# Attention's value products in three-half PSUM buffers, with a new order of the pieces

## The chip, the cores and the metric

The kernel runs on one core of one Trainium2 chip. What counts is the device time of one execution in microseconds (us), lower being better. All times below come from runs on the chip and from one execution that the hardware profiler recorded.

## What is computed

One layer of a decoder trunk for 1024 prompt tokens and 8 sample tokens with 1024 channels: a mixer (pooling and convolution), cross-attention to 256 memory tokens with 4 heads of 256 channels, and a gated feed-forward part. The change lies in the cross-attention:

```python
def cross_attn(h, k, v, w_q, w_o):
    B, L, _ = h.shape
    q = (h @ w_q).reshape(B, L, MEM_HEADS, MEM_HEAD_DIM)
    s = jnp.einsum('blhd,bmhd->bhlm', q, k).astype(jnp.float32) / math.sqrt(MEM_HEAD_DIM)
    p = jax.nn.softmax(s, axis=-1).astype(v.dtype)
    o = jnp.einsum('bhlm,bmhd->blhd', p, v).reshape(B, L, D_MODEL)
    return o @ w_o
```

The sample tokens have keys and values of their own (a cache), and the prompt's are computed from `mem_prompt`.

## The kernel before, in words

**Precision.** Each operand of a matmul is held as a pair, a rounded high part and a low part (the rest). A product is three passes (`PASSES`: high by high, high by low, low by high) into one PSUM accumulation. So a product's result leaves PSUM twice: ScalarE (ACT) copies it to the high part, and then VectorE (DVE) subtracts that copy from the same PSUM data to make the low part.

**Stages of the attention.** Letters name the pieces in the string `ORDER`, and a digit follows each. `q` is the query projection of 128 channels (72 matmuls, tile `ps`). `S` is the scores of 256 tokens of one head (12 matmuls into one bank, tile `sc`), with the softmax: maximum on DVE, exponentials on ACT, normalisation on GpSimd (POOL) or DVE (tile `probs`). `T` transposes four 128x128 blocks of probabilities on the TensorE (PE; tile `pt`), and ACT and DVE split them into the pair `pT`. `P` is the value product: `P`n makes output channels 128n to 128n+127 of the attention from head n//2 (tile `pv`, line 1083 on), in two halves of 512 tokens, c = 0 and 1. A half is six matmuls into one bank (lines 1091 to 1095). ACT's copy is line 1098 and DVE's subtraction line 1099, and both write halves of the pair `oo`n. `a`, `b`, `c`, `d`, `e` do the same for the samples without the PE's matmuls: DVE multiplies cache rows (`spcache_k`, `spcache_v`) by broadcast rows (`sbcache_k`, `sbcache_v`), which pass through DRAM (`qd` for queries, `pd` for the probabilities `prow`), and POOL writes the samples' columns of `oo` (lines 375 and 384). `o` is the output projection (tile `po`, line 485), which reads all eight `oo`.

**PSUM.** [...] Two buffers of three banks each (tag `mm`) serve `ps`, `pv`, `po` and some of the `sc`, in turn, and two of one bank each (tag `ms`) serve `pt`, most `sc` and small sums. A `pv` buffer holds the two halves of one `P`, so one of its three banks stays empty.

**Order.** Every piece adds tasks to a list, with what each reads and writes (`Program.add`). For PSUM those keys are finer than a tile: `(ps, c)` is one half. `Program.order` then plans all engines with costs of its own and writes the instructions out in the planned order; each engine runs its instructions in that order. The string `ORDER` sets the tasks' priorities, so a new string moves instructions on every engine. The waits between engines are put in by the layer below, which sees the instructions one after another in the planned order, with the tiles that they touch.

Of the kernel before, what the change touches and what calls it, by code (L numbers as in the profile page):

```python
# [10 lines left out]
AF = mybir.ActivationFunctionType  # L11
ALU = mybir.AluOpType
AX = mybir.AxisListType

P = 128
# [25 lines left out]
ORDER = (  # L41
# [5 lines left out]
)  # L47

# [5 lines left out]
ALL_SAMPLES = (1, 6, 7)  # L54

SCORES_MM = (12, 13, 14, 15)
SLACK = {"Pool": 0.3, "ACT": 0.15, "DVE": 0.05, "PE": 0.05}


# [16 lines left out]
A12, A22, S4, S1, A11, S2, S3 = range(7)  # L76
# [27 lines left out]
class Program:  # L104
# [10 lines left out]
    def add(self, engines, emit, r=(), w=(), lock=False, func=None, nbytes=0):  # L115
        t = Task()
        t.engines = {}
        for e, cost in engines.items():
            factor, more = self.margin.get(e, (1, 0)) if not nbytes else (1, 0)
            t.engines[e] = cost * factor + more  # L120
        t.emit, t.lock, t.func, t.nbytes = emit, lock, func, nbytes
        t.prio = len(self.tasks) + self.later
        if "PE" not in engines and any(isinstance(x[0], Buf) and x[0].tag in ("mm", "ms") for x in r):
            t.prio += BIAS["evac"]
        deps = set()
        for x in r:
            if x in self.writer:
                deps.add(self.writer[x])
        for x in w:
            if x in self.writer:  # L130
                deps.add(self.writer[x])
            deps.update(self.readers.get(x, ()))
        for x in r:
            self.readers.setdefault(x, []).append(t)
        for x in w:
            self.writer[x], self.readers[x] = t, []
        deps.discard(t)
        t.deps, t.followers, t.ends = deps, [], {}
        t.waiting = len(deps)
        for d in deps:  # L140
            d.followers.append(t)
        t.bufs = list({id(x[0]): x[0] for x in list(r) + list(w) if isinstance(x[0], Buf)}.values())
        self.tasks.append(t)
        return t

    def order(self):
# [48 lines left out]
        while len(issued) < len(self.tasks):  # L195
            best = None
            for e, tasks in open_.items():
                pick, slack = None, SLACK.get(e, 0.02)
                for t in tasks:
# [61 lines left out]
def hybrid_step_kernel(ctx: ExitStack, tc: tile.TileContext, io):  # L261
# [9 lines left out]
    add = pg.add  # L271

    def buf(name, tag, shape, dtype=F32):
        return Buf(name, tag, shape, dtype)

    def op_buf(name, shape=(P, 2, T), dtype=F32):
        return buf(name, "op", shape, dtype)
# [7 lines left out]
    def mm_buf(name, width=3):  # L285
        return buf(name, "mm", (P, width, 512))

    def ms_buf(name):
        return buf(name, "ms", (P, 512))

    def f32(ap):
        return ap.bitcast(F32)
# [8 lines left out]
    def pe(n, count=1):  # L301
        return (0.0135 + 0.000417 * n) * count
# [4 lines left out]
    def act(n, ps=False, ptrs=0):  # L307
        return (0.05 if ps else 0.093) + 0.000833 * n + 0.093 * ptrs

    def dve(n):  # L310
        return 0.065 + 0.00105 * n
# [493 lines left out]
    a2 = [op_buf(f"a{i}") for i in range(2)]  # L805
# [143 lines left out]
    x1 = [op_buf(f"x1_{j}") for j in range(4)]  # L949
# [60 lines left out]
    probs, pT = {}, {}  # L1010
# [8 lines left out]
    def scores(n):  # L1019
# [3 lines left out]
        pr = probs[h]  # L1023
        ps = mm_buf(f"sc{h}_{i2}", 1) if n in SCORES_MM else ms_buf(f"sc{h}_{i2}")
        pk = (ps,)
# [39 lines left out]
    def p_transpose(n):  # L1065
# [7 lines left out]
        def emit(e):  # L1073
# [6 lines left out]
        add({"DVE": dve(512)}, lambda e: e.tensor_tensor(pt[:, 1, sl], ps[:], f32(pt[:, 0, sl]), ALU.subtract),  # L1080
            [(ps,), (pt, 0, t4)], [(pt, 1, t4)])

    def pv(n):
        h, dt = n // 2, n % 2
        ps = mm_buf(f"pv{n}", 2)
        col, v = (h % 2) * 256 + dt * P, vv[h // 2]
        oo = oop[n]
        for c in range(2):
            sl = slice(c * 512, (c + 1) * 512)

            def emit(e, c=c, sl=sl):
                for m in range(2):
                    for p, (vi, pi) in enumerate(PASSES):
                        e.matmul(ps[:, c], v[:, vi, m, col : col + P], pT[h][m][:, pi, sl],  # L1094
                                 start=(m == 0 and p == 0), stop=(m == 1 and p == 2))

            add({"PE": pe(512, 6)}, emit, [(v, 0), (v, 1)] + [(pT[h][m], p, c) for p in range(2) for m in range(2)], [(ps, c)])
            add({"ACT": act(512, True)}, lambda e, c=c, sl=sl: e.activation(oo[:, 0, sl], ps[:, c], AF.Copy), [(ps, c)], [(oo, 0, c)])
            add({"DVE": dve(512)}, lambda e, c=c, sl=sl: e.tensor_tensor(oo[:, 1, sl], ps[:, c], f32(oo[:, 0, sl]), ALU.subtract),  # L1099
                [(ps, c), (oo, 0, c)], [(oo, 1, c)])  # L1100


    def s_query(h):
# [496 lines left out]
    def hidden_load(f):  # L1600
# [9 lines left out]
        "Y": lambda _: state_out("pool_s", st_pool, "pool", 15), "Z": lambda _: state_out("conv_s", st_conv, "conv", 30),  # L1610
        "L": lambda _: layer_norm(), "V": values, "O": pair(out_a), "B": pair(out_b),
        "q": q_group, "f": lambda _: token_factors(), "t": x1_square, "u": x2_square, "S": scores, "T": p_transpose, "P": pv,
        "a": s_query, "b": s_scores, "c": s_softmax, "d": s_values, "e": s_out,
        "o": proj_o, "x": lambda n: plain_block(A12 if n > 3 else A11, n % 4, n // 4, 0), "y": lambda j: plain_block(A22, j, 1, 1), "z": sum_blocks,
# [24 lines left out]
    for u in range(units):  # L1639
        c, p = u // 4, u % 4  # L1640
# [222 lines left out]
```

## Time and profile before

| | us |
|---|---|
| median of 3 runs (1216.54 to 1219.12) | 1217.39 |
| the profiled execution | 1217.88 |
| its span on the profile | 1216.1 |
| PE busy in it | 1198.4 |
| first `pv` matmul | 411.2 |
| first `po` matmul | 447.8 |

The span runs from the first instruction to the last. PE, DVE, ACT and POOL are the engines, PEld the weight loads of the PE, SPq the queue that issues most DMAs. Times in a timeline count from the span's start. "[1.15 <-DVE oo L1099]" behind a row means that the engine had been idle for 1.15 us, and that an instruction of line 1099 on DVE ended this.

### The profile page before, as it was taken

The numbers are of one execution on the slowest core, as the hardware profiler recorded it, in microseconds if no ns is written. First come the engines' busy times: TensorE is split into PE (matmuls) and PEld (weight loads), VectorE is DVE, ScalarE is ACT, GpSimd is POOL, SyncE is SP. The second block draws the span as 40 slices with busy tenths as digits, with TensorE's granted clock in tenths as the row PEclk, the third lists the DMA queues.
The fourth block names the chain that finished last, engine by engine and source line by source line (L and its number), as shares of the span: only waits on it lengthen the run. The fifth ranks groups of instructions, "written<-read, shape, count | busy, mean of one in ns | idle before, by whom it ended". The sixth has DMA issues, their size and how long they took to land.

```text
span 1216.1 us, 19401 instructions
## 1 busy us (share of the span) xinstructions
PE 1198.4 (99%) x7720; PEld 1121.8 (92%) x7720; DVE 930.1 (76%) x1548; ACT 524.7 (43%) x718; POOL 251.4 (21%) x297
## 2 busy tenths in 40 slices
PE   8999999999999999999999999999999999999997
PEld 7999988999999979999999999999999999999886
DVE  7999999766258886679877777777867798879744
ACT  7765656455135533454222322233222355544633
POOL 3568842231111102131000000000000024332101
PEclk9999999999999999999999999999999999999999
DMA  7335677326386774422332233222313597678612
GB/s 289 86 73 116 144 210 223 117 104 207 108 266 205 244 271 150 122 87 66 118 114 80 96 114 111 108 79 97 123 70 105 206 309 216 169 195 222 150 52 89
DMA packets 60170, 179.69 MB, mean 148 GB/s; under 512 B 7792, under 2 KB 11568, under 8 KB 58800
## 3 DMA queue, kind: packets, MB, share of 16 engines
q1 hardware_dynamic: 53824, 157.92, 37.4%
q0 software_dynamic: 6256, 20.54, 9.9%
q8 instruction: 60, 0.98, 0.3%
q14 instruction: 30, 0.25, 0.1%
HBM read 144.66 MB, written 33.78 MB: 147 GB/s over the span
## 4 chain that ended last, share of the span: by engine, by line
PE 78%; DVE 4%; DMA 1%; issue 1%; ACT 1%; POOL 0%; DVEq 0%; SPq 0%; ACTq 0%
PE pr L1339 48%; PE po L485 8%; PE fd L1682 6%; PE ps L485 5%; PE oa L485 4%; PE ob L485 4%; PE sc L1036 1%; DVE spcache_k L1133 1%; PE pv L1094 1%; DMA sbcache_v<-pd 1%; DVE oo L1099 1%; PE kps L860 0%; DVE pT L1080 0%; DMA raw<-in_w_k 0%; DMA pd<-prow 0%
## 5 line engine op out<-in xcount | busy, mean ns | idle before, releaser
L1339 PEld LDWEIGHTS pr<-ab,wTb 128*128 128x128 f32 x1056 | 131.8, 188 | 3.5
L1339 PE MATMUL pr<-ab,wTa 128*128 128x260 f32 x1056 | 133.6, 282 | 0.2 <-DVE su L1355 0.2
L1339 PE MATMUL pr<-ab,wTb 128*128 128x260 f32 x1056 | 133.0, 282 | 0.0
L1339 PEld LDWEIGHTS pr<-ab,wTa 128*128 128x128 f32 x1056 | 130.8, 188 | 2.4 <-DVE su L1355 0.4
L1339 PE MATMUL pr<-ab,wG 128*128 128x512 f32 x528 | 129.3, 393 | 0.0
L1355 DVE TENSOR_TENSOR su<-pr,su 128x520 f32<-128x520 f32 (+1 forms) x112 | 77.7, 695 | 57.9 <-PE pr L1339 57.7
L1339 PEld LDWEIGHTS pr<-ab,wG 128*128 128x128 f32 x528 | 96.3, 188 | 19.7 <-DVE wG L384 0.4
L485 PE MATMUL ps<-xop,w 128*128 128x344 f32 x720 | 114.1, 320 | 0.0
L485 PEld LDWEIGHTS ps<-xop,w 128*128 128x128 f32 x720 | 113.6, 188 | 0.0
L1339 PEld LDWEIGHTS pr<-hb,dV 128*128 128x128 f32 x768 | 98.8, 188 | 4.1
L1339 PE MATMUL pr<-hb,dV 128*128 128x260 f32 x768 | 100.1, 283 | 0.0
L485 PE MATMUL ps<-xq,w 128*128 128x344 f32 x576 | 94.9, 322 | 0.5 <-DMA w<-in_w_q 0.5
L485 PEld LDWEIGHTS ps<-xq,w 128*128 128x128 f32 x576 | 90.8, 188 | 0.9 <-DMA w<-in_w_q 0.8
L485 PEld LDWEIGHTS po<-oo,w 128*128 128x128 f32 x576 | 90.8, 188 | 0.6 <-DVE oo L1099 0.4
L485 PE MATMUL po<-oo,w 128*128 128x344 f32 x576 | 91.3, 320 | 0.0
L694 DVE SCALAR_TENSOR_TENSOR cacc<-glu,vec,cacc 128x511 f32<-128x511 f32 (+14 forms) x116 | 76.9, 744 | 0.0
L1339 PE MATMUL pr<-hb,dW 128*128 128x512 f32 x288 | 74.6, 394 | 0.0
L373 ACT ACTIVATE w<-raw 128x1024 fp32r<-128x1024 f32 (+1 forms) x37 | 34.9, 949 | 86.1 <-PE po L485 24.2
L1682 PE MATMUL fd<-ho,w 128*128 128x260 f32 (+1 forms) x432 | 69.1, 321 | 0.0
L1366 POOL MEMSET su<- 128x16 f32 x22 | 2.5, 112 | 318.9 <-PE pr L1339 267.7
L1682 PEld LDWEIGHTS fd<-ho,w 128*128 128x128 f32 x432 | 62.0, 188 | 6.9 <-issue 0.5
L1339 PE MATMUL pr<-ab,wU 128*128 128x512 f32 x264 | 64.6, 393 | 0.0
(309 smaller groups left out, 2189.2 us busy)
## 6 DMA issues: line engine op xcount, KB each, us to landing
gr<-in_w_gu SPq DMA_DIRECT2D x44, 512.0 KB, 3.7
hb<-su SPq DMA_DIRECT2D x8, 1040.0 KB, 4.6
hs<-hb SPq DMA_DIRECT2D x16, 520.0 KB, 5.1
dr<-in_w_dn SPq DMA_DIRECT2D x16, 512.0 KB, 4.6
spcache_k<-in_cache_k SPq DMA_DIRECT2D x12, 512.0 KB, 5.1
hs<-hb SPq DMA_DIRECT2D x12, 512.0 KB, 5.0
raw<-in_w_in SPq DMA_DIRECT2D x10, 512.0 KB, 3.7
hb<-he SPq DMA_DIRECT2D x8, 520.0 KB, 3.6
```

Of the source, the lines that this page charges most:

```text
L373: e.activation(dst(0), src(), AF.Copy, scale=1.0 if gain is None else gain)
L485: e.matmul(ps[:, c, :CW], w[:, wi, cols], x[:, xi, c * CW : (c + 1) * CW], start=first and p == 0, stop=last and p == 2)
L694: e.scalar_tensor_tensor(acc[h][:, n:], src[:, : HALF - n], w, acc[h][:, n:], ALU.mult, ALU.add)
L1036: e.matmul(bank()[:, i * NMEM : (i + 1) * NMEM], qop[2 * h + dt][:, qi, tt * P : (tt + 1) * P], kk[:, ki, 2 * (h % 2) + dt], start=(dt == ...
L1094: e.matmul(ps[:, c], v[:, vi, m, col : col + P], pT[h][m][:, pi, sl], start=(m == 0 and p == 0), stop=(m == 1 and p == 2))
L1099: add({"DVE": dve(512)}, lambda e, c=c, sl=sl: e.tensor_tensor(oo[:, 1, sl], ps[:, c], f32(oo[:, 0, sl]), ALU.subtract), [(ps, c), (oo, 0, ...
L1133: e.scalar_tensor_tensor(piece[:, b], piece[:, b], 1.0, bc[:, b], ALU.mult, ALU.mult, accum_out=out(m)[:, first + b : first + b + 1])
L1339: e.matmul(bank(c), w[:, wi, cols(j)], xs[0](j, xi)[:, c * n : (c + 1) * n], start=onto is None and j == 0 and p == 0, stop=j == nj - 1 an ...
L1355: from_sums(sums, "DVE", dve, lambda e, src, sl: e.tensor_tensor(as_banks(o(sl), src), src, as_banks(a(sl), src), op), [akey], [okey])
L1366: add({"Pool": 0.12}, lambda e: e.memset(o(), 0.0), [], keys)
L1682: e.matmul(view(i), w[:, wi, col : col + P], hops[k][:, xi, half, lo - half * HALF + i * width // count : lo - half * HALF + (i + 1) * wid ...
```

## The change

The function `pv` no longer takes a buffer for each `P`. It counts halves. The first, second and third of three successive halves go to banks 0, 1 and 2 of one buffer, and the fourth takes the next buffer. After `P1` (the constant `EARLY_PV`), which comes first and alone, the count starts anew. So `P1` has a buffer with two halves, and the other fourteen halves lie in five buffers: three, three, three, three and two, where they had seven. Matmuls, copies and subtractions stay as they were, and as many. `ORDER` is rewritten from `S2` to `P5`, and one piece (`z0`) moves ahead of `o2` behind it.

```diff
-    "S2 q4 q5 a2 Y0 S7 S1 S3 S8 T0 d0 T3 T4 S9 T1 S10 T2 d1 q6 T8 q7 S11 T11 T5 P1 S12 T10 a3 S15 S13 T9 S14 T12 b2 T7 T6 "
-    "T13 b3 T14 T15 c3 c2 d2 P4 e1 e0 P5 P2 P3 P7 d3 P0 e3 P6 e2 o0 u0 o4 o1 o5 x1 u4 u1 u5 h0 x0 x4 y0 o2 z0 x5 h2 h3 u2 "
+    "S2 q5 S3 q4 Y0 S1 T0 d0 a2 T1 S8 S10 S11 T2 T3 d1 q6 S9 q7 T8 S7 P1 T10 T4 b2 T7 a3 T5 S12 S13 T11 T12 S15 e0 T6 S14 "
+    "T14 T13 T9 c2 b3 e1 d2 c3 T15 e2 P2 d3 e3 P4 P0 P3 P7 P6 P5 o0 u0 o4 o1 o5 x1 u4 u1 u5 h0 x0 x4 y0 z0 o2 x5 h2 h3 u2 "
...
+EARLY_PV = 1
...
+    pv_banks = {"next": 0}
+
     def pv(n):
         h, dt = n // 2, n % 2
-        ps = mm_buf(f"pv{n}", 2)
...
         for c in range(2):
             sl = slice(c * 512, (c + 1) * 512)
-
-            def emit(e, c=c, sl=sl):
+            bank = pv_banks["next"] % 3
+            if not bank:
+                pv_banks["ps"] = mm_buf(f"pv{n}_{c}")
+            ps = pv_banks["ps"]
+            pv_banks["next"] += 1
+
+            def emit(e, sl=sl, ps=ps, bank=bank):
                 for m in range(2):
                     for p, (vi, pi) in enumerate(PASSES):
-                        e.matmul(ps[:, c], v[:, vi, m, col : col + P], pT[h][m][:, pi, sl],
+                        e.matmul(ps[:, bank], v[:, vi, m, col : col + P], pT[h][m][:, pi, sl],
                                  start=(m == 0 and p == 0), stop=(m == 1 and p == 2))
...
+        if n == EARLY_PV:
+            pv_banks["next"] = 0
```

The places below show the instructions as they stand in the built programs. A number behind a name tells buffers apart, "x3" is three in a row, and what a row waits for stands in brackets, by the engine whose count it waits on.

**The PE before, `P3` and `P7`.** Each has a buffer of its own (`pv3`, `pv7`), and its two halves are rows of three and three matmuls each.

```order
L1146 MATMUL ss2_4289<-ident_74,ssc_81 8x128
L1094 MATMUL pv3_4294<-pT1_0_3836,vv0_2016 128x512 [waits DVE_49]
L1094 MATMUL pv3_4294<-pT1_0_3836,vv0_2016 128x512 x2
L1094 MATMUL pv3_4294<-pT1_1_4182,vv0_2016 128x512 x3
L1094 MATMUL pv3_4294<-pT1_0_3836,vv0_2016 128x512 x3
L1094 MATMUL pv3_4294<-pT1_1_4182,vv0_2016 128x512 x3
L1094 MATMUL pv7_4322<-pT3_0_4200,vv1_1805 128x512 [waits DVE_49]
L1094 MATMUL pv7_4322<-pT3_0_4200,vv1_1805 128x512 x2
```

Each buffer is begun with a wait for DVE, and the second half has none.

**The PE after the change, the same products and the next.** `pv3_0` holds both halves of `P3` and the first of `P7`, `pv7_1` the second of `P7` and both of `P6`, and `pv5_0` both of `P5`.

```order
L1101 MATMUL pv3_0_4296<-pT1_0_4085,vv0_2016 128x512 x3
L1101 MATMUL pv3_0_4296<-pT1_1_4116,vv0_2016 128x512 x3
L1101 MATMUL pv3_0_4296<-pT3_0_4182,vv1_1805 128x512 [waits Activation_49]
L1101 MATMUL pv3_0_4296<-pT3_0_4182,vv1_1805 128x512 x2
L1101 MATMUL pv3_0_4296<-pT3_1_4212,vv1_1805 128x512 x3
L1101 MATMUL pv7_1_4335<-pT3_0_4182,vv1_1805 128x512 [waits DVE_49]
L1101 MATMUL pv7_1_4335<-pT3_0_4182,vv1_1805 128x512 x2
L1101 MATMUL pv7_1_4335<-pT3_1_4212,vv1_1805 128x512 x3
L1155 MATMUL ss3_4345<-ident_74,ssc_81 8x128 [waits DVE_49,PE_49]
L1155 MATMUL ss3_4345<-ident_74,ssc_81 8x128 [waits DVE_49]
L1101 MATMUL pv7_1_4335<-pT3_0_4182,vv1_1805 128x512 x3
L1101 MATMUL pv7_1_4335<-pT3_1_4212,vv1_1805 128x512 x3
```

A buffer is still begun with a wait for DVE, and its third half now has one for ACT (`pv7_1`'s as well, in the next rows).

**The PE after the change, from the last products to the output projection.** The first row is `pv7_1`'s third half.

```order
L1101 MATMUL pv7_1_4335<-pT3_0_4182,vv1_1805 128x512 [waits Activation_49]
L1101 MATMUL pv7_1_4335<-pT3_0_4182,vv1_1805 128x512 x2
L1101 MATMUL pv7_1_4335<-pT3_1_4212,vv1_1805 128x512 x3
L1101 MATMUL pv5_0_4375<-pT2_0_4025,vv1_1805 128x512 [waits DVE_49]
L1101 MATMUL pv5_0_4375<-pT2_0_4025,vv1_1805 128x512 x2
L1101 MATMUL pv5_0_4375<-pT2_1_4067,vv1_1805 128x512 x3
L1101 MATMUL pv5_0_4375<-pT2_0_4025,vv1_1805 128x512 x3
L1101 MATMUL pv5_0_4375<-pT2_1_4067,vv1_1805 128x512 x3
L486 MATMUL po0_4401<-oo0_4013,w44_3813 128x344 [waits DVE_49]
```

The projection's first matmul waits for DVE, as before, where the two halves ahead of it were those of `P6`; the buffer that it takes is the one that `pv7_1` had, since the two are used in turn.

**DVE after the change, behind the last products.** `sst3` and `prow3` are the softmax of the samples' fourth head, `oo`n the subtractions.

```order
L1106 TENSOR_TENSOR oo7_4342<-pv3_0_4296,oo7_4342 128x512
L1106 TENSOR_TENSOR oo7_4342<-pv7_1_4335,oo7_4342 128x512 [waits Activation_49]
L1171 RECIPROCAL sst3_4355<-sst3_4355 8x1
L1172 TENSOR_SCALAR prow3_4361<-prow3_4361,sst3_4355 8x256 [waits DMAHW2_49,DVE_49]
L1106 TENSOR_TENSOR oo6_4370<-pv7_1_4335,oo6_4370 128x512
L1106 TENSOR_TENSOR oo6_4370<-pv7_1_4335,oo6_4370 128x512 [waits Activation_49]
L1106 TENSOR_TENSOR oo5_4397<-pv5_0_4375,oo5_4397 128x512 [waits Activation_49] x2
```

Before, `prow3` had four subtractions behind it, those of `P0` and `P6`. Now there are four again, `P6` and `P5`, but ahead of it stands the subtraction of a half that shares its buffer with the next two.

More of the change, by code (lines that the diff above doesn't have):

```diff
@@ L1089, in pv @@
             sl = slice(c * 512, (c + 1) * 512)
-            def emit(e, c=c, sl=sl):
+            bank = pv_banks["next"] % 3
[4 more added lines that the diff above has]
+            def emit(e, sl=sl, ps=ps, bank=bank):
                 for m in range(2):
                     for p, (vi, pi) in enumerate(PASSES):
-                        e.matmul(ps[:, c], v[:, vi, m, col : col + P], pT[h][m][:, pi, sl],
+                        e.matmul(ps[:, bank], v[:, vi, m, col : col + P], pT[h][m][:, pi, sl],
                                  start=(m == 0 and p == 0), stop=(m == 1 and p == 2))
[L1097 to L1100, printed above, removed]
+            add({"PE": pe(512, 6)}, emit, [(v, 0), (v, 1)] + [(pT[h][m], p, c) for p in range(2) for m in range(2)], [(ps, bank)])
+            add({"ACT": act(512, True)}, lambda e, sl=sl, ps=ps, bank=bank: e.activation(oo[:, 0, sl], ps[:, bank], AF.Copy), [(ps, bank)], [(oo, 0, c)])
+            add({"DVE": dve(512)}, lambda e, sl=sl, ps=ps, bank=bank: e.tensor_tensor(oo[:, 1, sl], ps[:, bank], f32(oo[:, 0, sl]), ALU.subtract),
+                [(ps, bank), (oo, 0, c)], [(oo, 1, c)])
+        if n == EARLY_PV:
+            pv_banks["next"] = 0
     def s_query(h):
```

## The prediction

> **What bounds the kernel now.** I read the page's busy times first, then a table of stretches around the attention, then PE's waits, and last the timeline of the stretch in which the `pv` products run.
>
> ```profile
> span 1216.1 us, 19401 instructions
> PE 1198.4 (99%) x7720; PEld 1121.8 (92%) x7720; DVE 930.1 (76%) x1548; ACT 524.7 (43%) x718; POOL 251.4 (21%) x297
> core 0: us, PE busy (x) PEld busy (x) DVE busy (x) ACT busy (x) POOL busy (x), PEclk, DMA share, GB/s
> 375.00:411.00 36.00, 36.00 (x259) 35.81 (x258) 29.27 (x110) 16.68 (x40) 5.29 (x8) 1.00 0.61 200
> 411.00:426.00 15.00, 14.57 (x101) 12.55 (x100) 13.19 (x34) 12.15 (x31) 2.11 (x7) 1.00 0.88 291
> 426.00:434.00 8.00, 8.00 (x43) 6.59 (x42) 6.81 (x24) 4.35 (x8) 0.00 (x0) 1.00 0.14 53
> 434.00:448.00 14.00, 12.62 (x55) 9.33 (x54) 11.31 (x35) 5.76 (x13) 0.00 (x0) 1.00 0.89 325
> 448.00:460.00 12.00, 12.00 (x77) 12.00 (x78) 9.68 (x49) 1.05 (x2) 0.87 (x4) 1.00 1.00 404
> 540.00:560.00 20.00, 19.83 (x111) 16.13 (x110) 18.74 (x28) 12.87 (x21) 9.41 (x9) 1.00 0.22 80
> ```
>
> PE sets the time. It is idle for 17.7 us of the span (1216.1 - 1198.4). The change leaves every matmul as it is, so it can act only on those gaps. In the stretch that it rewrites, 375 to 448, PE is idle for 0.43 + 1.38 us, and a little more, since ends of matmuls are modelled. So even a perfect result is worth some 2 us, and a loss has no such bound.
>
> ```profile
> PE pv L1094 <- DVE oo L1099: 1.4, 2, 1.2
> 377.24 0.22 PE sq L1108 x2
> 434.16 0.38 PE L1146 MATMUL ss<-ident,ssc 128*8 128x128 f32 x2
> 435.70 5.84 PE L1094 MATMUL pv<-pT,vv 128*128 128x512 f32 x24 [1.15 <-DVE oo L1099]
> 440.64 1.29 DVE L1099 TENSOR_TENSOR oo<-pv,oo 128x512 fp32r<-128x512 f32 x2
> 441.37 0.38 PE L1146 MATMUL ss<-ident,ssc 128*8 128x128 f32 x2
> 441.57 1.09 ACT L1098 ACTIVATE oo<-pv 128x512 fp32r<-128x512 f32 x2 [1.71 <-PE pv L1094]
> 441.99 5.83 PE L1094 MATMUL pv<-pT,vv 128*128 128x512 f32 x24 [0.23 <-DVE oo L1099]
> 447.82 3.42 PE L485 MATMUL po<-oo,w 128*128 128x344 f32 x20
> ```
>
> The gaps are waits for a buffer: PE may begin `P3` only when DVE has made the last subtraction from the buffer of `P5`, and so on. The reader should see three of them. Two small transposes like `ss` take 0.22 (the `sq` row), so PE was ready at 434.38 and 441.59 and went on at 435.70 and 441.99: 1.32 and 0.40. Four halves last from 435.70 to 441.37, 5.67, so 1.42 each. The last four end at 441.99 + 5.67 = 447.66, and `po` begins at 447.82: 0.16.
>
> **What is removed.** With six banks in turn instead of four, a buffer is waited for three halves after its own last one, and not two. `pv3_0` begins when the two halves and a transpose that follow `pv2_0` are through, and so on down to `pv5_0`; each subtraction then has at least one half more of cover, 1.42 against the longest wait of 1.32. I count the three waits as gone: -1.88.
>
> **What is added: the third half waits for ACT.** The built program has PE wait for ACT ahead of the third half of all four full buffers. The trace tells what such a wait costs.
>
> ```profile
> 423.18 1.67 PE L1094 MATMUL pv<-pT,vv 128*128 128x512 f32 x6
> 425.80 1.64 PE L1094 MATMUL pv<-pT,vv 128*128 128x512 f32 x6
> 427.28 0.60 PE L1075 MATMUL pt<-ident,probs 128*128 128x128 f32 x4
> 427.48 1.09 ACT L1098 ACTIVATE oo<-pv 128x512 fp32r<-128x512 f32 x2 [0.80 <-PE pv L1094]
> 427.63 1.65 PE L1094 MATMUL pv<-pT,vv 128*128 128x512 f32 x6
> 447.86 0.60 ACT L1098 ACTIVATE oo<-pv 128x512 fp32r<-128x512 f32 x1 [0.82 <-PE pv L1094]
> 448.49 0.69 DVE L1099 TENSOR_TENSOR oo<-pv,oo 128x512 fp32r<-128x512 f32 x1 [0.73 <-ACT oo L1098]
> 449.21 0.60 ACT L1098 ACTIVATE oo<-pv 128x512 fp32r<-128x512 f32 x1 [0.76 <-DVE oo L1099]
> 449.84 0.69 DVE L1099 TENSOR_TENSOR oo<-pv,oo 128x512 fp32r<-128x512 f32 x1 [0.66 <-ACT oo L1098]
> ```
>
> `P4`'s first half is the row at 423.18, its second the one at 425.80. ACT stood idle for 0.80 and copied the first half only at 427.48, when the second was done. So a copy waits for what stands ahead of it in the order for the same buffer, not for its own bank, though the planner's keys are by bank. By the same rule a third half that stands behind the first copy waits for this copy, and the copy for the second half: PE stops after the second half until one copy is through. The copy starts 0.20 after PE goes on (427.28 to 427.48, 441.37 to 441.57) and takes 0.60, and a release reaches PE 0.06 later (440.64 + 1.29 = 441.93 to 441.99). So 0.86 a third half. Three have nothing on PE between second and third half: 2.58. In `pv2_0` four transposes stand between, 0.35 (427.28 to 427.63): 0.51. Bounds: 0 if the copy named is an old one, 1.35 a half if it is the second copy, 0.49 later (1.09 for two in a row, less 0.60). I take the first copy, since the rows have just that pattern. Behind PE's wait stand the rest of the products, so the whole row of copies and subtractions moves with it.
>
> **What is added: the projection's first buffer.** `po0` takes the buffer of `pv7_1`, with only the two halves of `pv5_0` in between, 2.84. After the end of `pv7_1`'s third half come a copy (0.20 and then 447.86 to 448.49, 0.63), DVE's subtraction for `oo7`, the end of the samples' softmax, and the chain of subtraction, copy, subtraction for `oo6` (448.49 to 450.53, 2.04).
>
> ```profile
> 442.69 1.29 DVE L1099 TENSOR_TENSOR oo<-pv,oo 128x512 fp32r<-128x512 f32 x2 [0.26 <-ACT oo L1098]
> 443.90 0.14 DVE L1162 RECIPROCAL sst<-sst 8x1 f32<-8x1 f32 x1
> 444.07 0.34 DVE L1163 TENSOR_SCALAR prow<-prow,sst 8x256 f32<-8x256 f32 x1
> 444.44 0.29 SPq L359 DMA_DIRECT2D pd<-prow  x1
> 448.26 0.32 SPq L359 DMA_DIRECT2D sbcache_v<-pd  x1
> 457.23 0.43 DVE L1133 SCALAR_TENSOR_TENSOR spcache_v<-spcache_v,sbcache_v 128x256 f32<-128x256 f32 x1 [1.17 <-DMA sbcache_v<-pd]
> 463.22 0.20 POOL L384 TENSOR_TENSOR oo<-qs,oo 128x8 fp32r<-128x8 f32 x1
> 447.82 91.25 PE po L485 x576
> ```
>
> Two subtractions take 1.21 (442.69 to 443.90), so one 0.60; the reciprocal and `prow` 0.54 (443.90 to 444.44). Together 0.20 + 0.63 + 0.60 + 0.54 + 2.04 + 0.06 = 4.07, less 2.84: +1.23. Bounds: 0.1, if the first subtraction and the softmax are done before that half ends, and 1.7 with the second copy's 0.49 on top.
>
> **What is moved.** From 375 to 411 PE is busy throughout with the `q` projections, 11 us each, and what moves there (`S`, `T`, the samples' `qrow` and their issues on SP) has these to hide behind: 0. Without that cover a score's softmax would be in the open, as in 411 to 426, where PE follows DVE. There one normalisation of `probs` passes from DVE to POOL, and of the transposes one more than before, eleven, stands behind `P1`, among the products.
>
> ```profile
> 419.81 0.62 DVE probs L1061 x2
> ```
>
> That is up to 0.62 of DVE's chain. I take -0.40, with -1.0 and +0.5 as ends, since the split of the added transpose, which DVE shares, comes later and other pieces change places there. On SP the broadcast for the samples' fourth head of keys passes two loads of the value cache, and two `xa` loads pass the `pd` of the fourth head: what DVE needs first goes first, 0. POOL's weight DMA stands behind the same PE matmuls. From 448 to 460 PE has no gap, and at 540 to 560 only 0.17, so `z0` ahead of `o2` is 0 as long as the projections (91.25 for 576 matmuls) cover it.
>
> **The sum:** -1.88 + 2.58 + 0.51 + 1.23 - 0.40 = +2.04. The profiled execution took 1217.88 around its span, so 1219.92 by it; the median shown is 0.49 lower, so 1217.39 + 2.04 = **1219.4 us**, 0.17% slower. Within 0.2% (2.43 us) a measurement of this kernel can't tell a change from none.
>
> **Rivals.**
>
> *The third half does not wait in fact.* The awaited copy would be long done, or the waits be by bank. Then behind `pv7_1`'s third half only one copy and one subtraction are left, 0.20 + 0.63 + 0.69 = 1.52, which 2.84 hide, and the sum is -1.88 - 0.40: 1215.1 us. For it speaks that the planner counts by bank; against it the copy at 427.48, which waited for a bank that it doesn't read. It decides if PE's gap ahead of third halves is under about 0.2. [...]
>
> *DVE paces the products either way.* From 411 to 448 DVE has 31.31 us of work in 37. If it is the true bound, a PE wait taken away comes back as another, and third-half waits fall into time that PE would have waited anyway: 1217.4 us. Against it: from 426 to 434 PE has no gap beside a DVE busy for 6.81 of 8.
>
> *The samples' fourth head comes late.* Its probabilities go through DRAM (444.44), a broadcast (448.26 to 457.23), DVE's products and POOL, which ends at 463.42. PE takes that column in the projection's matmul 124: 447.82 + 123 x 0.158 = 467.3, so 3.8 us are spare. In the new order `prow3` stands 1.25 us nearer to `po0` (3.75 before, now 0.34 + 2.04 + 0.12) and PE takes the column six matmuls earlier, 0.95: 1.6 left. If the broadcast, with the DMA engines full (1.00 at 404 GB/s), takes over 1.6 us longer, each further one costs one; 2 us more make 1221.4. Against it: two `xa` loads of the four that were queued ahead of the broadcast now go out before.
>
> **How the numbers follow.** The forecast 0.72, waits gone in fact 0.05, DVE paces 0.08, the fourth head late 0.12, anything else slower 0.03. The forecast's own range is 1218.2 to 1221.0: the early pieces +-0.6, `po0`'s term down by 1.1 or up by 0.5, each third half 0.1 either way. Its middle lies just inside 0.2%, its upper side is the longer one, and I give 0.34 to inside and 0.38 to slower. With the rivals: slower 0.38 + 0.12 + 0.03 = 0.53; within 0.34 + 0.08 + 0.02 = 0.44; faster 0.03, the lower part of the first rival. The range from 1216.8 to 1222.0 leaves out that rival and the end of the third.
>
> **What would show it.** In the changed kernel's waits, PE `pv` behind ACT `oo` four times for 0.5 to 0.9 us, and no longer behind DVE `oo` among the products; ahead of `po` a gap of 1 us or more, ended by DVE `oo`. The first `po` matmul moves from 447.8 to about 449.9, and everything behind by the same. If no gap names ACT, the second step is wrong; if `po`'s first gap is under 0.3, the third is; if PE stops within `po` at the samples' columns, the last rival holds.

## The result, and the profile after

The changed kernel takes 1222.3 us (median of 9 runs, 1221.1 to 1227.27), the kernel before 1217.92 (9 runs beside them, 1216.54 to 1219.23). The ratio is 1.0036 with a 95% interval from 1.0028 to 1.0044: slower by 4.4 us. The forecast was 2.0 us slower, with a range that ends 0.3 below the result. The direction was right and the size half of what came.

The page of the changed kernel, span and busy times:

```profile
span 1221.1 us, 19399 instructions
PE 1199.1 (98%) x7720; PEld 1121.4 (92%) x7720; DVE 930.5 (76%) x1549; ACT 524.6 (43%) x718; POOL 249.8 (20%) x296
```

PE has the same matmuls and the same busy time to 0.7 us; the span grew by 5.0. So it is idle time of PE, and PE's waits from 360 to 480 us in the changed kernel name it (engine and line that waits, what ended the wait, us in total, times, the longest; the four largest):

```profile
PE pv L1101 <- ACT oo L1105: 2.3, 4, 0.7
PE po L486 <- DVE oo L1106: 1.1, 1, 1.1
PE sc L1037 <- DVE pT L1081: 0.6, 1, 0.6
PE pt L1076 <- DVE probs L1062: 0.6, 1, 0.6
```

The first two rows are what the prediction asked for: `pv` behind ACT's copy four times, the projection behind DVE's subtraction once, and no `pv` behind DVE any more. The last two were not foreseen. They lie ahead of the first `pv`, where I had put the price at nothing.

To see what each stretch contributes, I take four landmarks that are the same matmuls in every kernel: the first scores, the first value product, the first projection and the first product of the next stage. First the kernel before, then the changed one, from PE's timelines (start, duration, engine, line, operation):

```profile
349.54 1.58 PE L1036 MATMUL sc<-kT,qo 128*128 128x256 f32 x12
411.20 2.94 PE L1094 MATMUL pv<-pT,vv 128*128 128x512 f32 x12
447.82 91.26 PE L485 MATMUL po<-oo,w 128*128 128x344 f32 x576
538.91 5.99 PE L1339 MATMUL pr<-ab,wG 128*128 128x512 f32 x24
```

```profile
350.32 1.57 PE L1037 MATMUL sc<-kT,qo 128*128 128x256 f32 x12
413.22 2.96 PE L1101 MATMUL pv<-pT,vv 128*128 128x512 f32 x12
452.34 91.18 PE L486 MATMUL po<-oo,w 128*128 128x344 f32 x576 [1.12 <-DVE oo L1106]
543.35 6.00 PE L1348 MATMUL pr<-ab,wG 128*128 128x512 f32 x24
```

From `sc` to `pv` 61.66 became 62.90, from `pv` to `po` 36.62 became 39.12, from `po` to `pr` 91.09 became 91.01: +1.24, +2.50, -0.08. The other 1.3 us of the difference of the spans lie ahead of the first scores (0.78) and behind `pr` (0.56), where PE has the same matmuls in the same order in both kernels; single executions scatter there by that much (the stretch behind `pr` took 675.9 to 678.6 us in the ten profiles of this study), and the distance of the medians, 4.4, is the better figure for the whole.

So there are two losses. Between `pv` and `po`, the prediction's terms added up to +2.04, and +2.50 came. Ahead of `pv` it had 0, and +1.24 came with one transpose fewer in that stretch (0.36 on PE, 437.39 to 437.75 in the changed kernel), so 1.6 us of loss. DVE's timeline of the changed kernel shows what ended late there, and PE's timeline below it what waited:

```profile
388.62 0.42 DVE L1142 SCALAR_TENSOR_TENSOR spcache_v<-spcache_v,sbcache_v 128x256 f32<-128x256 f32 x1 [2.48 <-DMA spcache_v<-in_cache_v]
390.01 1.28 DVE L1081 TENSOR_TENSOR pT<-pt,pT 128x512 fp32r<-128x512 f32 x2
407.14 0.43 DVE L1142 SCALAR_TENSOR_TENSOR spcache_k<-spcache_k,sbcache_k 128x256 f32<-128x256 f32 x1 [1.88 <-DMA spcache_k<-in_cache_k]
410.96 0.61 DVE L1062 TENSOR_SCALAR probs<-probs,sm 128x256 f32<-128x256 f32 x2
```

```profile
390.75 1.45 PE L1037 MATMUL sc<-kT,qo 128*128 128x256 f32 x10 [0.60 <-DVE pT L1081]
411.37 0.59 PE L1076 MATMUL pt<-ident,probs 128*128 128x128 f32 x2 [0.58 <-DVE probs L1062]
```

DVE ran its instructions in the planned order. It reached a multiplication of cache rows at 386.14 and went on 2.48 us later, when the rows had landed; the subtraction of `pT` that PE waited for stood behind it. The same again at 405.26 with rows of the keys, 1.88 us, and the normalisation of `probs` behind them. These rows were not loaded later than before. SP's queue, first in the kernel before and then in the changed one:

```profile
384.70 0.81 SPq L359 DMA_DIRECT2D spcache_v<-in_cache_v  x2
```

```profile
383.46 1.01 SPq L360 DMA_DIRECT2D spcache_v<-in_cache_v  x2
```

The loads went out 1.2 us earlier. But in the kernel before DVE came to these rows 4.4 us after the issue, when they were there, if only just: they had landed 4.3 us after it.

```profile
389.07 0.43 DVE L1133 SCALAR_TENSOR_TENSOR spcache_v<-spcache_v,sbcache_v 128x256 f32<-128x256 f32 x1
```

In the changed one it came 2.7 us after the issue (383.46 to 386.14), they landed after 5.1, and DVE went on at 388.62.

The keys are another case. Their loads, the first two of the four in each row, also went out earlier; first the kernel before, then the changed one:

```profile
402.51 7.64 SPq L359 DMA_DIRECT2D spcache_k<-in_cache_k  x4
```

```profile
400.51 10.63 SPq L360 DMA_DIRECT2D spcache_k<-in_cache_k  x4
```

In the kernel before DVE came to the first of them 4.45 us after its issue and had no wait:

```profile
406.96 0.42 DVE L1133 SCALAR_TENSOR_TENSOR spcache_k<-spcache_k,sbcache_k 128x256 f32<-128x256 f32 x1
```

In the changed one it came after 4.75 us (405.26), so no sooner behind the issue. Here the load itself took longer: 6.5 us, where before it was there within 4.45. It went out 1.4 us behind the broadcast of the same head's query (`sbcache_k`, issued at 399.07), before 3.4 us behind it (399.14), and from 400 to 403 us the DMA engines were busy for 0.86 of the time in place of 0.53. Whether that slowed it, no run tests. In the kernel before no wait of DVE between 366 and 414 us ended with a DMA.

### The profile page after: what moved, and what is told of

Its sections match the earlier page's. It is cut to its first block, busy times and chain, and to the rows that moved or that the text cites. A ratio compares the mean times of both kernels' runs of the same rounds, so it can differ in the third digit from the quotient of the medians.

```text
span 1221.1 us, 19399 instructions
## 1 busy us (share of the span) xinstructions
PE 1199.1 (98%) x7720; PEld 1121.4 (92%) x7720; DVE 930.5 (76%) x1549; ACT 524.6 (43%) x718; POOL 249.8 (20%) x296
## 4 chain that ended last, share of the span: by engine, by line
PE 91%; DVE 4%; DMA 2%; issue 1%; ACT 1%; SPq 0%; DVEq 0%; ACTq 0%
PE pr L1348 48%; PE ps L486 14%; PE po L486 7%; PE fd L1691 6%; PE oa L486 4%; PE ob L486 4%; PE kps L861 2%; PE vps L938 2%; PE pv L1101 2%; PE sc L1037 1%; DMA w<-in_w_q 1%; PE pmap L881 1%; DMA spcache_k<-in_cache_k 1%; DMA xraw<-in_xT 1%; DVE w L385 0%
```

## The experiments

**Theory:** the 4.4 us are two losses, about 2 us from the packing (third halves behind ACT, the projection's first buffer) and about 2 us from the new order ahead of `pv0`, where DVE stands behind cache rows that have not landed. **Rivals:** (A) all of it is the packing's; (B) the order matters only with the packing; (C) the packing alone gains, and the order undid it; (D) in the stretch ahead of `pv` not the loads set the time but the two PSUM buffers that the softmax tiles share; (E) the third half's wait only moves elsewhere if it is taken away.

The landmarks of all profiles, in us from one to the next, and the medians with the ratio to the kernel before on the same chip (its medians: 1217.45 beside the first four, 1218.07 beside the next three, 1218.63 beside the last):

| kernel | `sc` to `pv` | `pv` to `po` | `po` to `pr` | median | ratio, 95% |
|---|---|---|---|---|---|
| before | 61.66 | 36.62 | 91.09 | 1217.92 | |
| changed | 62.90 | 39.12 | 91.01 | 1222.30 | 1.0028 to 1.0044 |
| 1 order alone | 62.26 | 42.24 | 93.58 | 1228.00 | 1.0069 to 1.0095 |
| 2 packing alone | 61.99 | 39.64 | 95.32 | 1226.63 | 1.0057 to 1.0083 |
| 3 loads planned later | 61.05 | 42.97 | 95.38 | 1227.58 | 1.0071 to 1.0097 |
| 4 copies behind all halves | 62.63 | 39.38 | 91.00 | 1219.70 | 1.0015 to 1.0035 |
| 5 no wait for the rows | 61.06 | 39.01 | 91.02 | 1220.53 | 1.0015 to 1.0033 |
| 6 order alone, pause filled | 63.15 | 42.29 | 90.98 | 1223.33 | 1.0028 to 1.0053 |
| 7 as 4, old order up to `pv` | 62.36 | 41.46 | 92.51 | 1225.68 | 1.0053 to 1.0078 |
| 8 as 3 and 4 together | 61.46 | 39.71 | 92.47 | 1223.14 | 1.0028 to 1.0056 |

### 1 and 2: the order alone, the packing alone

The first is the kernel before with the change's string, the second the changed kernel with the old one:

```diff
 ORDER = (
...
-    "S2 q4 q5 a2 Y0 S7 S1 S3 S8 T0 d0 T3 T4 S9 T1 S10 T2 d1 q6 T8 q7 S11 T11 T5 P1 S12 T10 a3 S15 S13 T9 S14 T12 b2 T7 T6 "
-    "T13 b3 T14 T15 c3 c2 d2 P4 e1 e0 P5 P2 P3 P7 d3 P0 e3 P6 e2 o0 u0 o4 o1 o5 x1 u4 u1 u5 h0 x0 x4 y0 o2 z0 x5 h2 h3 u2 "
+    "S2 q5 S3 q4 Y0 S1 T0 d0 a2 T1 S8 S10 S11 T2 T3 d1 q6 S9 q7 T8 S7 P1 T10 T4 b2 T7 a3 T5 S12 S13 T11 T12 S15 e0 T6 S14 "
+    "T14 T13 T9 c2 b3 e1 d2 c3 T15 e2 P2 d3 e3 P4 P0 P3 P7 P6 P5 o0 u0 o4 o1 o5 x1 u4 u1 u5 h0 x0 x4 y0 z0 o2 x5 h2 h3 u2 "
```

> The kernel before (two halves to a buffer) with the change's order of pieces. My theory: the change's +4.4 us are about 2.0 us from the order ahead of `pv0` (DVE stands behind cache rows that land late, at 388 and 407 us) and about 2.1 us from the packing. Then this kernel is 1.5 to 3 us slower than before, its first `pv` matmul comes at about 413.2 us as in the changed kernel, and DVE shows the two waits for cache rows. Rival A, all the loss is the packing's: within 0.5 us of before, first `pv` at 411.2. Rival B, the order matters only together with the packing: the same as before, but with the waits seen.

> The changed kernel (three halves to a buffer) with the old order of pieces. My theory: no late cache rows, so the first `pv` matmul comes at 411.2 us as before; the third halves wait for ACT's first copy in at least three of four buffers (0.7 us each) and the first `po` for a release (about 1 us), while the 1.9 us of waits behind DVE are gone: +0.5 to +2.5 us against before. Rival A, all the loss is the packing's: +4 us or more. Rival C, the packing alone is worth what its removed waits were (the order undid it): -1 us or less.

Each part alone costs more than both together: +10.6 and +9.2 us by the medians. That fits no account that I had written down: neither +1.5 to 3 and +0.5 to 2.5, nor rivals A, B or C. Something can be read from them all the same. With the order alone DVE has the two waits for cache rows between 366 and 414 us, 1.9 and 1.8 us; with the packing alone it has one of 0.5. The stretch ahead of `pv` is longer with the order alone, too (62.26, and 63.15 in experiment 6, to 61.66), though a transpose fewer stands in it. So this loss comes with the order, in either packing, and A and B are out. C is out too, since the packing alone lengthens the stretch from `pv` to `po`, from 36.62 to 39.64.

In the first, PE stops ahead of the projection, and what DVE does there is in its timeline:

```profile
454.41 7.76 PE L485 MATMUL po<-oo,w 128*128 128x344 f32 x31 [3.80 <-DVE oo L1099]
```

```profile
447.45 0.41 DVE L1133 SCALAR_TENSOR_TENSOR spcache_v<-spcache_v,sbcache_v 128x256 f32<-128x256 f32 x1
...
452.98 2.48 DVE L1099 TENSOR_TENSOR oo<-pv,oo 128x512 fp32r<-128x512 f32 x4
```

Sixteen multiplications of cache rows, 5.5 us from 447.45 to 452.98, stand ahead of the four subtractions that free the projection's buffer. With the same string and buffers of three the planner puts these multiplications behind the subtractions. So the planner answers the string and the packing each by moving other work.

In the second, the third halves wait as in the changed kernel, and a wait within the projection is new:

```profile
PE pv L1101 <- ACT oo L1105: 2.6, 4, 0.7
PE po L486 <- POOL w L385: 1.9, 1, 1.9
```

```profile
475.45 1.07 POOL L398 TENSOR_SCALAR w<-raw 128x1024 fp32r<-128x1024 f32 x1 [6.55 <-PE po L486]
```

The weights take two buffers in turn. In this program the first one is in use until the 138th of the first 144 `po` matmuls (until the 120th in the changed kernel), so ACT begins the next weights in it at 474.45 in place of 471.62. The second is in use until the 144th, and the first step of preparing its next weights, which ACT makes in the changed kernel, went to POOL. That is the row above, at 475.45, and it stands ahead of POOL's subtraction for the first buffer (line 385), which so ran from 476.48 to 478.85 in place of 472.76 to 475.17. PE waited 1.89 us for it.

Both lost time in one more way, which the last section takes up: behind the pause PE ran for a while at half its clock (granted 0.50, for 6.8 us in the first and 3.4 us in the second). In sum, two kernels that share a plan with neither parent can't split the loss. The next experiments keep the plan fixed where that can be done.

### 3: the planner told of late rows

```diff
-                    P * count * 1024, w=[(piece,)])
+                    (LOAD_FACTOR if number in (2, 5) else 1) * P * count * 1024, w=[(piece,)])
```

with `LOAD_FACTOR = 2.5`.

> The changed kernel; only the planner is told that the pieces of two heads' cache rows (values of head 1, keys of head 2) take 2.5 times as long to land, so that DVE's subtraction of `pT` and its normalisation of `probs` stand ahead of the multiplications that waited for them. My theory: PE's waits at 390 and 411 us (0.60 and 0.58 us) and what hangs on them go, the first `pv` comes 1 to 2 us earlier than 413.2, and the time is 1 to 2 us under the changed kernel's (+2.4 to +3.4 against before). Rival D, the softmax tiles' two PSUM buffers and not the loads set that stretch: the waits for `pT` and `probs` move to other releasers, time within 0.5 us of the changed kernel's.

The waits ahead of `pv` went, and the stretch from `sc` to `pv` fell by 1.85 us against the changed kernel's (62.90 to 61.05), as the theory has it. The total did not: it is 5.3 us above the changed kernel's. The two longest of PE's waits from 360 to 490 us:

```profile
PE po L486 <- POOL w L385: 1.9, 1, 1.9
PE sc L1037 <- ACT probs L1054: 1.8, 1, 1.8
```

The first is the wait for the projection's weights from experiment 2 (the 138th matmul and POOL's order again), the second a new one among the last scores. Besides, `pv` waits 1.4 us for DVE's `oo`, and PE runs at half its clock twice (0.50, for 3.4 us each time; last section). So the mechanism holds, and its size in the total stays open here, since the plan moved.

### 4: copies behind all halves of a buffer

In the changed kernel a copy is added behind its own half. Here the copies and subtractions of a buffer are kept back until all its halves are there, and each depends on all its banks, so a third half never stands behind a copy of the same buffer:

```diff
-            add({"ACT": act(512, True)}, lambda e, sl=sl, ps=ps, bank=bank: e.activation(oo[:, 0, sl], ps[:, bank], AF.Copy), [(ps, bank)], [(oo, 0, c)])
+            pv_banks["late"].append((oo, sl, ps, bank, c))
+            if bank == 2 or (n in (EARLY_PV, LAST_PV) and c):
+                late, pv_banks["late"] = pv_banks["late"], []
+                filled = [(x[2], x[3]) for x in late]
+                for oo_, sl_, ps_, bank_, c_ in late:
+                    add({"ACT": act(512, True)}, lambda e, oo=oo_, sl=sl_, ps=ps_, bank=bank_: e.activation(oo[:, 0, sl], ps[:, bank], AF.Copy), filled, [(oo_, 0, c_)])
...
```

> The changed kernel with the copies and subtractions of a packed buffer put behind all its halves, so that the third half is issued ahead of the first copy and waits for nothing. My theory: the rows of PE's `pv` that end behind ACT's `oo` go (2.3 us in the changed kernel), the stretch from the first `pv` to the first `po` shortens by 1.5 to 2.5 us, and the time is +1.5 to +3 us against before. Rival E, the wait only moves (copies that start later release the buffer later, so that the next buffer but one waits for DVE): `pv` waits behind DVE's `oo` of 2 us or more, time as the changed kernel's or slower.

PE's waits in the products and at the projection:

```profile
PE po L486 <- ACT oo L1110: 1.2, 1, 1.2
PE ss L1160 <- DVE spcache_k L1147: 1.0, 1, 1.0
PE pv L1101 <- DVE oo L1111: 0.3, 1, 0.3
```

No `pv` waits for ACT any more, and the kernel stands 2.25 us above the one before by the medians (1219.70 to 1217.45), where the changed one stands 4.4 above: within the +1.5 to +3 of the theory. Rival E holds in small: a transpose of the samples' scores now waits 1.0 us for DVE, and `pv` 0.3 behind it. The projection's wait of 1.2 stays, and so do the two ahead of `pv`, 0.6 and 0.3, behind the late cache rows. The stretch from `pv` to `po` is not shorter in the profile, 39.38 to 39.12, against the theory. That execution took 1222.18, 2.5 us above the median of the 11 (1218.49 to 1224.12), and in it PE's clock was 0.50 from 441.6 to 445.1 us, so that the stretch holds this loss too.

### 5: the same plan without the wait for the rows

```diff
-                            e.scalar_tensor_tensor(piece[:, b], piece[:, b], 1.0, bc[:, b], ALU.mult, ALU.mult,
+                            rows, factor = (bc, 0.0) if number in (2, 5) else (piece, 1.0)
+                            e.scalar_tensor_tensor(rows[:, b], rows[:, b], factor, bc[:, b], ALU.mult, ALU.mult,
                                                    accum_out=out(m)[:, first + b : first + b + 1])
```

> The changed kernel, with the same instructions in the same order on every engine; only the multiplications of two heads' cache rows (values of head 1, keys of head 2) read the broadcast factors alone, so that DVE no longer waits there for the rows to land. The products of these two heads with the cache are left out of the result. My theory: DVE's waits for cache rows at 388 and 407 us and PE's gaps of 0.60 and 0.58 us behind them go, the first `pv` comes 1.2 to 2 us earlier, and the time is 1.2 to 2 us under the changed kernel's (+2.4 to +3.2 against before). Rival D, PSUM's softmax tiles set that stretch: the gaps stay behind another releaser, the time within 0.5 us of the changed kernel's.

Every engine has the changed kernel's instructions in the changed kernel's order. One thing moves along: the loads of these rows have no reader to wait for, and go out earlier (the row at 383.46 us begins at 378.22). PE's waits from 360 to 480 us are down to two rows, and the landmarks follow:

```profile
PE pv L1101 <- ACT oo L1105: 2.3, 4, 0.7
PE po L486 <- DVE oo L1106: 1.1, 1, 1.1
```

```profile
348.94 1.57 PE L1037 MATMUL sc<-kT,qo 128*128 128x256 f32 x12
410.00 2.97 PE L1101 MATMUL pv<-pT,vv 128*128 128x512 f32 x12
```

From `sc` to `pv` 61.06, 1.84 less than in the changed kernel; from `pv` to `po` 39.01, as there. The median falls by 1.8, from 1222.3 to 1220.53. This settles the second loss: the wait for cache rows in DVE's queue, 1.8 us. Rival D is out, since with the same PSUM buffers in the same order the gaps are gone and no other releaser took their place. What is left against the kernel before is 1220.53 - 1218.07 = 2.5 us by the medians (ratio 1.0024, 1.0015 to 1.0033). It is the packing's part together with what else the new order does; from `pv` to `po`, where the packing acts, it is 39.01 - 36.62 = 2.4.

### 6: the first experiment's pause filled

The kernel of experiment 1, with every engine's order as it was; the 12 matmuls write a bank that nobody reads, for which the buffers of `pv` get their third bank:

```diff
-        ps = mm_buf(f"pv{n}", 2)
+        ps = mm_buf(f"pv{n}")
...
+                if n == 5 and c == 1:
+                    for k in range(12):
+                        vi, pi = PASSES[k % 3]
+                        e.matmul(ps[:, 2], v[:, vi, k // 6, col : col + P], pT[h][k // 6][:, pi, sl], start=k == 0, stop=k == 11)
```

> The first experiment's kernel (old packing, new order), in which PE paused 3.80 us ahead of `po` and then ran at a granted clock of 0.50 from 453 to 460 us; the one difference are 12 matmuls of the size of `pv`'s (about 2.9 us) at the end of the last `pv` half, into a PSUM bank that nobody reads, so that PE is busy through most of the pause. Theory of the clock: the pause is what halves it; the clock stays at 1.00 and the time is 2 to 3.5 us under the first experiment's. Rival: the low clock comes from something else in that stretch (the DMA engines run at a share of 1.0 there); it stays, and the time is within 0.5 us of the first experiment's or above it.

The first `po` comes as long after the first `pv` as without the added matmuls (42.29 against 42.24), so they lie wholly within the pause, which has 1.08 us left. What follows the pause differs. Granted clock by the microsecond (stretch, its length, PE busy, count, clock, DMA share, GB/s), first in experiment 1, then with the pause filled:

```profile
453.00:454.00 1.00, 0.00 (x0) 0.73 0.97 410
454.00:455.00 1.00, 0.59 (x2) 0.50 0.98 407
...
459.00:460.00 1.00, 1.00 (x6) 0.50 0.54 206
460.00:461.00 1.00, 1.00 (x7) 0.86 0.28 116
```

```profile
454.00:455.00 1.00, 0.10 (x1) 1.00 0.96 399
...
459.00:460.00 1.00, 1.00 (x8) 1.00 0.71 281
```

With PE kept busy the clock stayed at 1.00, at a DMA share of 0.96 in place of 0.98 from 454 to 455 us, so the pause is what halved it, and the rival is out. From `po` to `pr` it takes 90.98 in place of 93.58: the half clock cost 2.6 us. The medians differ by 4.7, more than expected. In the two profiles the other 2.6 us lie behind `pr` (675.9 us to the end against 678.5), of which 0.60 is one wait of PE in experiment 1. The rest, 2.0, is spread evenly over the matmuls there, the same ones in the same order, which took 0.3% longer in experiment 1's execution at a granted clock of 1.00. So it is not the pause's doing; its cause is open.

### 7 and 8: two attempts to lose neither

The seventh has experiment 4's packing, the old order up to the first `pv` and the new one behind it; the eighth joins the edits of 3 and 4.

```diff
-    "S2 q5 S3 q4 Y0 S1 T0 d0 a2 T1 S8 S10 S11 T2 T3 d1 q6 S9 q7 T8 S7 P1 T10 T4 b2 T7 a3 T5 S12 S13 T11 T12 S15 e0 T6 S14 "
+    "S2 q4 q5 a2 Y0 S7 S1 S3 S8 T0 d0 T3 T4 S9 T1 S10 T2 d1 q6 T8 q7 S11 T11 T5 P1 T10 b2 T7 a3 S12 S13 T12 S15 e0 T6 S14 "
```

> Three halves to a buffer with copies and subtractions behind all halves of a buffer (no third half waits), and the old order of pieces up to `pv0`/`pv1` with the new one behind it (no late cache rows). Theory: the first `pv` comes as early as in the kernel before, `pv` waits for no `oo`, the first `po` waits about 1.2 us: -1 to +1 us against before. Rival E: the order behind `pv0` costs by itself what the fourth run showed there (a transpose of the scores waiting 1.0 us for DVE's cache work, and a half clock after it): +1.5 us or more.

> The third and the fourth experiment together: the planner is told that the cache rows of two heads land late, and a packed buffer's copies and subtractions stand behind all its halves. Theory: both losses of the changed kernel go together; the first `pv` comes as early as in the third experiment, no `pv` waits for ACT's `oo`, and the samples' scores' transpose, which waited 1.0 us in the fourth, now stands behind a `pv` half more. Then -1 to +1 us against before. Rival: as in the third and seventh experiment, the planner's new plan brings a pause of over 1.5 us at another place (DVE's cache work ahead of an `oo` subtraction, or the weights of `po` late, since the first weights' slot is held to the 135th of the first 144 `po` matmuls), with a half clock after it: +4 us or more.

Neither beats the kernel before: +7.6 and +4.5 us. In the seventh it is again DVE's queue, here in its own timeline:

```profile
445.65 0.41 DVE L1147 SCALAR_TENSOR_TENSOR spcache_v<-spcache_v,sbcache_v 128x256 f32<-128x256 f32 x1
...
451.18 3.07 DVE L1111 TENSOR_TENSOR oo<-pv,oo 128x512 fp32r<-128x512 f32 x5
```

Sixteen multiplications, 5.5 us, ahead of five subtractions, and the projection waits:

```profile
PE po L486 <- DVE oo L1111: 5.1, 1, 5.1
```

A `pv` waits another 1.7 us for DVE's `oo`, and behind the long wait the clock is 0.50 for 3.4 us.

The eighth came as its rival said. The third halves no longer wait, the first `pv` is early, and the planner's plan has pauses elsewhere, experiment 3's among them; a half clock behind them, which the rival had too, is not in the profile (the granted clock is 1.00 in every window from 400 to 600 us):

```profile
PE sc L1037 <- ACT probs L1054: 1.8, 1, 1.8
PE po L486 <- DVE oo L1111: 1.6, 1, 1.6
PE po L486 <- POOL w L385: 1.0, 1, 1.0
```

A version that is faster than the kernel before was not found; the nearest is experiment 4.

## Why the prediction was wrong, and where it was right

**Removed, -1.88: right.** No `pv` of the changed kernel waits for DVE. No run measures what that alone is worth.

**The third half, +3.09: right in cause and close in size.** Four waits for ACT, of 0.25 (430.10), 0.69, 0.69 and 0.69. Each costs some 0.16 more than its idle time, since two PE rows that follow each other directly overlap in the records (in the changed kernel one ends at 435.91 + 1.65 = 437.56, and the next begins at 437.39). So 0.85 where I had 0.86, and 0.41 where I had 0.51. Experiment 4 shows that it is the order within the buffer that makes them wait: with the copies behind all halves, no `pv` waits for ACT, with the same banks in use. The rival by which banks decide fell with that.

**The projection's first buffer, +1.23: right.** 1.12 of idle time and the 0.16 of overlap make 1.28, ended by DVE as said.

**The early pieces, -0.40: not borne out.** From `pv` to `po` the kernel has lost 2.50. The waits make 2.96 + 1.28 - 1.88 = 2.36, and the transpose that now stands in this stretch 0.36, so 0.2 came back at most; nothing shows what the normalisation that passed to POOL gave.

**What is moved, 0: wrong, and this is the step that failed.** The prediction said that what moves between 375 and 411 has the `q` projections to hide behind, and of SP's queue that "what DVE needs first goes first, 0". PE being busy there hides only what is not needed by PE itself. I looked at when loads are issued, and not at when DVE reaches the instruction that needs them and what stands behind it. The new order brought DVE to two groups of rows 2.48 and 1.88 us before it could go on with them, with `pT` and `probs` behind them, and PE had no slack for either. For the values it came sooner after the issue than before, for the keys the load took longer. So the term was not 0; experiment 5 measures it: 1.8 us. With it in the sum, +2.04 + 1.8 = +3.8, 1221.2 us, which is within 1.1 us of the result. The prediction also held that within 0.2% a change can't be told from none; with nine runs of each kernel the interval, 1.0028 to 1.0044, lies wholly above that.

**The rivals on record.** The third half waits in fact. DVE does not pace the products, since its release no longer ends any wait of a `pv`. Within `po` the changed kernel has no stop, so the samples' fourth head was in time; experiments 2, 3 and 8 show a stop at that place of another kind, for weights.

**What stays open:** why the order alone gained 4.7 us by filling a pause whose half clock accounts for 2.6, why the keys took longer to land, and where the 1.1 us above come from. A half clock is not among their causes in the profiled execution, which has none between 360 and 1200 us (1.00 in every window of 2 us).

## What to carry to other kernels

A busy PE hides moved work only as long as nothing that PE needs stands behind it (here such work cost 1.8 us, experiment 5): for each load, compare the moment at which the engine that runs its instructions in order reaches its first use (2.7 us after the issue for DVE and the values) with issue plus landing (5.1 us), and then look at what is queued behind that use. Leave room in the landing: equal loads of cache rows, 512 KB each, took from 4.0 to 7.4 us in the changed kernel between 370 and 405 us. When a planner places the work, half of a change is another plan, and not half of the effect; two parts that lost 10.6 and 9.2 us alone lost 4.4 together. An edit that leaves every engine's order as it was (other operands, or matmuls into an unused bank) tells causes apart where a reordered kernel can't.

## What the runs showed of the hardware

In experiments 1, 2, 3, 4 and 7 PE's granted clock went to 0.50 in a pause or up to 1.5 us behind one, for 6.8 us in experiment 1 and for 3.4 us each time in the others. Meanwhile matmuls took longer. The first 31 of `po` took 7.76 us in experiment 1, where the clock was at 0.50 until about 460.3 us, and 5.15 us in the kernel before. The 12 of `sc` behind a pause of 1.83 us took 2.45 us in experiment 3, where the clock fell 0.6 us after they began, and 1.68 us in experiment 8 behind an equal pause, at 1.00. In experiment 3 there are two such stretches in one execution; here in windows of one microsecond, with the columns as above:

```profile
423.00:424.00 1.00, 1.00 (x8) 0.56 0.51 164
424.00:425.00 1.00, 1.00 (x6) 0.50 0.78 279
...
426.00:427.00 1.00, 1.00 (x5) 0.73 0.83 221
...
481.00:482.00 1.00, 1.00 (x6) 0.57 1.03 421
482.00:483.00 1.00, 1.00 (x5) 0.50 1.01 411
...
484.00:485.00 1.00, 1.00 (x6) 0.72 1.07 221
```

These lengths are estimates from such windows: taking the clock as either 1.00 or 0.50 at any moment, which are its values in the whole microseconds on both sides of a fall or rise, a mean of 0.56 over a microsecond at whose end the clock is 0.50 means 0.88 us at 0.50, so it fell at 423.12; 0.73 means 0.54 us, so it rose at 426.54: 3.42 us. The second goes from 481.14 to 484.56, 3.42 as well. The length of a pause alone didn't decide. Pauses that a half clock went with: 1.83 us and, in a second place, 1.87 with 0.47 shortly ahead (experiment 3), 1.89 with 0.47 shortly ahead (experiment 2), 1.02 and 0.33 with 0.27 between them (experiment 4), 3.80 (experiment 1, 6.8 us of half clock) and 5.13 (experiment 7, 3.4 us). Pauses without one: 1.12 in the changed kernel, 1.47 in experiment 1, 1.71 in experiment 7, and 1.83 in experiment 8.
